# Order of weight sums, loads and block differences in the weight preparation of a hybrid decoder step

## The chip, the cores and the metric

The kernel runs on one core of one Trainium2 chip. The metric is the device time of one execution in microseconds (us). A core has a matrix engine (TensorE, PE), a vector engine (VectorE, DVE), a scalar engine (ScalarE, ACT), a general engine (GpSimd, POOL) and a sync engine (SyncE, SP), which here issues most transfers. Each engine executes its own instructions in order; between engines, semaphores order the work.

## The reference

One inference step of a one-layer decoder trunk, for a prompt group (512 tokens) and a sample group (8 x 8 tokens), 576 columns in all. D_MODEL is 1024, a branch is 512 wide, the MLP 4096.

```
h = _rmsnorm(x, g_mix_pre)
rq, rk, rv, rg, aq, ak, av, cb, cc, ch, gates = _split_in(h @ w_in)
o_ret, ret_new = _retention_branch(rq, rk, rv, rg, ret_s0)
if win_k is None:
    o_att, wk_new, wv_new = _attn_prompt(aq, ak, av, sinks)
else:
    o_att, wk_new, wv_new = _attn_sample(aq, ak, av, win_k, win_v, sinks)
o_conv, conv_new = _short_conv_branch(cb, cc, ch, conv_buf, conv_w)
branches = jnp.stack([o_ret, o_att, o_conv], axis=2)
proj = jnp.einsum('btnw,nwd->btnd', branches, w_branch)
gate = jax.nn.sigmoid(gates.reshape(b, t, N_BRANCH, d))
mixed = jnp.sum(gate * proj, axis=2) @ w_out
x = x + _rmsnorm(mixed, g_mix_post)
f = jnp.square(jax.nn.relu(_rmsnorm(x, g_ffn_pre) @ w_ff1)) @ w_ff2
x = x + _rmsnorm(f, g_ffn_post)
x = x + jax.nn.sigmoid(_rmsnorm(x, g_ple) @ w_ple_gate) * (p_l @ w_ple_proj)
```

## The kernel before

All activations are kept transposed, 576 columns in two halves of H = 288. Weights come as tiles W[j] of 128 x 1024 (eight 128 x 128 blocks, 512 KB). Each float32 operand is split into a rounded high part and the remainder, its low part: ACT casts the high part (`whi`, line 256), DVE subtracts it from the raw tile for the low part (`wlo`, line 257). A product is then three matmuls: high x high, high x low, low x high (`product`, line 329).

Most weights are used in pairs of tiles by Strassen's scheme with seven products instead of eight. A pair has four blocks of 128 x 512, b11, b12, b21, b22, and four sums of them:

```
t3 = b12 + b22      t2 = b11 + t3      t1 = b12 + b11      t4 = t2 + b21
```

For some pairs ("ready") the sums lie in DRAM already, summed there by accumulating transfers that POOL issues a few at a time after each `tick` (line 262 ff.); for the other pairs, here called plain, DVE adds them on the chip (line 227, 128 x 512, 90 instructions). `Pair.prep` is a generator with four pieces: b11 and t3; t2 and b21; t1 and b22; t4. Each piece loads, adds, casts, subtracts, and yields. For a plain pair the raw tile c holds W[j] = b12, b22 (512 KB), r holds b11, t3 and s holds t2, b21; t1 is written over b12 in c, t4 over t2 in s. The raw tiles rotate through four buffers (two pools of two).

The stream of products (`pair`, `pairs`) calls `step()` at fixed places, and each call advances the preparation of a coming tile by one piece. `pump()` does the same for the background work of the branches (retention, attention; lines 686 to 1040). A pair's products fill three PSUM banks: pa, pbb and pe. `value` (lines 418 to 427) reads two of the four results as differences: c21 = pe - hlf (line 424), c22 = hlf - pbb (line 426). The last product of a pair (b22) accumulates into pbb, so PE can begin it only after line 426 has read that bank. The order on each engine follows from the order of the program and the framework's scheduler, which honours priorities; the loads are issued by SP in its order, and each waits until its raw buffer is released.

Lines that the argument names: 390, 396, 400 copies of a pair on ACT; 424, 426 differences on DVE; 562, 690, 691 end of the retention's normalization on DVE, before which a power is taken on POOL (555) and read by 556; 721 a matmul that needs 690; 844 short convolution; 892 to 902 softmax of the sample attention, 1017 the transposes that need its result; 974 and 964 the same for the prompt.

Of the kernel before, what the change touches and what calls it, by code (L numbers as in the profile page):

```python
# [7 lines left out]
F32 = mybir.dt.float32  # L8
F32R = mybir.dt.float32r
AF = mybir.ActivationFunctionType  # L10
ALU = mybir.AluOpType
# [6 lines left out]
H = 288  # L18
# [66 lines left out]
def decoder_step(ctx: ExitStack, tc: tile.TileContext, xT, pT, W, consts, smalls, s0q, s0t, ckT, cv,  # L85
                 yT, o_rp, o_rs, o_akT, o_avT, o_ck, o_cv, o_conv):
    nc = tc.nc
    V, A, G, PE = nc.vector, nc.scalar, nc.gpsimd, nc.tensor
# [81 lines left out]
    def wtile(n):  # L170
        ph, pl = whi, wlo
        if n < 8:
            ph = pl = wparts[npart[0] % len(wparts)]
            npart[0] += 1
        return (ph.tile([P, n, P], F32R, tag="whi", name=nm("whi")), pl.tile([P, n, P], F32R, tag="wlo", name=nm("wlo")))
# [4 lines left out]
    def rawtile():  # L180
        pool = rawpools[nraw[0] % len(rawpools)]
        nraw[0] += 1
        return pool.tile([P, 8, P], F32, tag="wst", name=nm("wst"))
# [25 lines left out]
    def load(dst, src):  # L209
        nc.sync.dma_start(out=dst.rearrange("p k m -> p (k m)"), in_=src)  # L210

    class Pair:
# [7 lines left out]
        def prep(self, j):  # L220

            ready = j in sums
            t3, t2, t1, t4 = sums.get(j, [None] * 4)
            b12, b22, b11, b21 = [W[j + q // 2][:, Q * (q % 2):Q * (q % 2) + Q] for q in range(4)]

            def add(out, a, b):
                V.tensor_tensor(out=out, in0=a, in1=b, op=ALU.add)  # L227

            raw = []
            for i, parts in enumerate(((("b11", b11), ("t3", t3)), (("t2", t2), ("b21", b21)),  # L230
                                       (("t1", t1), ("b22", b22)), (("t4", t4),))):
                n = 4 * len(parts)
                if ready or i < 2:
                    r = rawtile()
                    raw.append(r)
                if ready:
                    for k, (name, src) in enumerate(parts):
                        load(r[:, 4 * k:4 * k + 4, :], src)
                elif i == 0:
                    c = rawtile()  # L240
                    load(c, W[j])
                    load(r[:, :4, :], b11)
                    add(r[:, 4:, :], c[:, :4, :], c[:, 4:, :])
                elif i == 1:
                    load(r[:, 4:, :], b21)
                    add(r[:, :4, :], raw[0][:, :4, :], raw[0][:, 4:, :])
                elif i == 2:
                    r = c
                    add(r[:, :4, :], r[:, :4, :], raw[0][:, :4, :])
                else:  # L250
                    r = raw[1]
                    add(r[:, :4, :], r[:, :4, :], r[:, 4:, :])
                hi, lo = wtile(n)
                for k, (name, _) in enumerate(parts):
                    self.w[name] = (hi, lo), 4 * k
                A.copy(out=hi, in_=r[:, :n, :])  # L256
                V.tensor_tensor(out=lo, in0=r[:, :n, :], in1=hi.bitcast(F32), op=ALU.subtract)  # L257
                if i % 2 == 0:
                    tick(hi)
                yield  # L260

    wsums = [weight_sums()]
    pace = cpool.tile([P, 1], F32, name="pace")
# [153 lines left out]
    def value(q, which, out):  # L417

        if which == "c11":
            return q.a[:, :H]  # L420
        if which == "c12":
            return q.b[:, :H]
        if which == "c21":
            V.tensor_tensor(out=out, in0=q.e[:, :H], in1=q.es, op=ALU.subtract)
        else:
            V.tensor_tensor(out=out, in0=q.es, in1=q.b[:, :H], op=ALU.subtract)  # L426
        return out

    def where(which):
# [186 lines left out]
    raw = []  # L616
# [728 lines left out]
    for c in range(1, 4):  # L1345
# [3 lines left out]
        n = 4 if c < 3 else 2  # L1349
# [140 lines left out]
```

## Time and profile before

| | before |
|---|---|
| three runs, median | 987.39 us (986.63 to 988.03) |
| the profiled execution | 987.22 us, span 985.4 us |
| PE busy | 957.6 us, 97% of the span, 7081 matmuls |
| DVE busy | 712.6 us, 72%, 1308 instructions |
| ACT busy | 531.5 us, 54% |
| POOL busy | 187.1 us |
| chain that ended last | PE 77%, DVE 13%, DMA 4%, ACT 2%, issue 2% |

The chain is followed back from the last instruction, at each step to what released it. PE's 77% of it is the part in which PE waited for nothing; the rest are places where the chain runs through other engines. A line in the profile is a line of the kernel; line 227 is the weight sum, 256 the cast, 257 the subtraction.

### The profile page before, as it was taken

How to read it: one execution, taken by the hardware profiler on the slowest of the kernel's cores; microseconds unless marked ns; L12 is line 12 of the kernel's file. 1: busy time of each engine (PE TensorE's matmuls, PEld its weight loads, DVE VectorE, ACT ScalarE, POOL GpSimd, SP SyncE). 2: the span in 40 equal slices, each digit the busy share in tenths (PEclk: the TensorE clock that was granted, in tenths of full speed). 3: DMA queues.
4: the chain of work that ended last, by engine and by line, in shares of the span. 5: the costliest groups of instructions: out<-in, count | busy, mean ns of one | idle time of the engine just before them, and what ended most of it. 6: DMA issues, size and time to landing. Idle time of an engine off the chain costs nothing.

```text
span 985.4 us, 18290 instructions
## 1 busy us (share of the span) xinstructions
PE 957.6 (97%) x7081; PEld 925.0 (94%) x7081; DVE 712.6 (72%) x1308; ACT 531.5 (54%) x1051; POOL 187.1 (19%) x257
## 2 busy tenths in 40 slices
PE   9999999989989999999999999999999999999998
PEld 9999898989979888799999999999999999999897
DVE  7898789765576776577427878558847965785986
ACT  7345444433345564545436455468558845885642
POOL 0414443433324222332001100000010011000010
PEclk9999999999999999999999999999999999999999
DMA  8637565658779665688522532444486368593112
GB/s 301 168 86 199 165 138 146 163 164 220 194 218 248 143 153 153 143 226 252 187 66 71 223 108 100 155 148 145 120 199 192 110 153 222 164 356 109 65 62 79
DMA packets 65576, 160.45 MB, mean 163 GB/s; under 512 B 8089, under 2 KB 11193, under 8 KB 64241
## 3 DMA queue, kind: packets, MB, share of 16 engines
q1 hardware_dynamic: 48672, 114.75, 34.9%
q0 software_dynamic: 16672, 44.48, 21.8%
q8 instruction: 55, 0.90, 0.4%
q14 instruction: 33, 0.26, 0.1%
q10 hardware_dynamic: 144, 0.06, 0.0%
HBM read 139.17 MB, written 51.55 MB: 194 GB/s over the span
## 4 chain that ended last, share of the span: by engine, by line
PE 77%; DVE 13%; DMA 4%; ACT 2%; issue 2%; POOL 1%; SPq 0%; ACTq 0%; DVEq 0%; POOLq 0%
PE pm L501 31%; PE pbb L329 18%; PE pa L329 12%; PE pe L329 12%; DMA wst<-in_W 3%; DVE wlo L257 3%; POOL rs_b L555 1%; DVE hlf L1149 1%; DVE xl L579 1%; DVE x L1150 1%; DVE wst L227 1%; DVE s L952 1%; PE pb L964 1%; ACT whi L256 1%; DVE wlo L164 1%
## 5 line engine op out<-in xcount | busy, mean ns | idle before, releaser
L257 DVE TENSOR_TENSOR wlo<-wst,whi 128x1024 fp32r<-128x1024 f32 (+1 forms) x180 | 195.4, 1087 | 95.9 <-ACT whi L256 95.1
L256 ACT CAST whi<-wst 128x1024 fp32r<-128x1024 f32 (+1 forms) x180 | 168.3, 940 | 129.9 <-PE pe L329 29.9
L329 PE MATMUL pbb<-xs,whi 128*128 128x288 f32 x1080 | 227.1, 302 | 10.0 <-DVE akv L426 4.1
L329 PEld LDWEIGHTS pbb<-xs,whi 128*128 128x128 f32 x1080 | 174.9, 190 | 19.0 <-DVE akv L426 4.9
L329 PE MATMUL pbb<-xs,wlo 128*128 128x288 f32 x540 | 160.6, 297 | 0.0
L329 PE MATMUL pa<-fq,whi 128*128 128x288 f32 x720 | 147.7, 297 | 0.6 <-DVE fq L583 0.5
L329 PEld LDWEIGHTS pa<-fq,whi 128*128 128x128 f32 x720 | 116.0, 189 | 2.3 <-DVE fq L583 0.7
L329 PE MATMUL pa<-fq,wlo 128*128 128x288 f32 x360 | 106.8, 297 | 0.4 <-DVE wlo L257 0.4
L329 PEld LDWEIGHTS pbb<-xs,wlo 128*128 128x128 f32 x540 | 102.7, 190 | 0.0
L163 ACT CAST whi<-wst 128x1024 fp32r<-128x1024 f32 (+1 forms) x64 | 61.5, 965 | 70.9 <-PE pm L501 48.8
L501 PE MATMUL pm<-xl,whi 128*128 128x288 f32 x384 | 95.0, 299 | 1.5 <-DVE xl L579 1.4
L501 PE MATMUL pm<-xh,whi 128*128 128x288 f32 x384 | 94.9, 300 | 1.5 <-ACT xh L578 1.4
L501 PE MATMUL pm<-xh,wlo 128*128 128x288 f32 x384 | 93.5, 296 | 0.3 <-DVE wlo L164 0.3
L164 DVE TENSOR_TENSOR wlo<-wst,whi 128x1024 fp32r<-128x1024 f32 (+1 forms) x64 | 71.2, 1118 | 23.7 <-ACT whi L163 21.3
L268 POOL COPY pace<-whi 128x1 f32<-128x1 f32 x61 | 36.6, 600 | 240.8 <-ACT whi L256 190.3
L227 DVE TENSOR_TENSOR wst<-wst 128x512 f32<-128x512 f32 x90 | 61.1, 686 | 28.7 <-DMA wst<-in_W 28.0
L555 POOL TENSOR_TENSOR rs_b<-rs_a,mhalf 128x9 f32<-128x9 f32 (+2 forms) x15 | 34.8, 2322 | 222.7 <-DVE rs_a L554 222.7
L329 PE MATMUL pe<-xs,whi 128*128 128x288 f32 x360 | 73.5, 294 | 0.1
L329 PE MATMUL pe<-fq,whi 128*128 128x288 f32 x360 | 73.3, 296 | 0.0
L501 PE MATMUL pm<-fq,whi 128*128 128x288 f32 x384 | 70.4, 296 | 0.0
L329 PEld LDWEIGHTS pa<-fq,wlo 128*128 128x128 f32 x360 | 67.9, 189 | 1.9 <-DVE wlo L257 1.1
L501 PEld LDWEIGHTS pm<-xh,whi 128*128 128x128 f32 x384 | 65.7, 188 | 3.9 <-ACT xh L578 2.4
(280 smaller groups left out, 2025.6 us busy)
## 6 DMA issues: line engine op xcount, KB each, us to landing
wst<-in_W SPq DMA_DIRECT2D x86, 512.0 KB, 4.5
wst<-in_W SPq DMA_DIRECT2D x105, 256.0 KB, 3.3
ts<-in_W POOLq DMA_DIRECT2D x90, 256.0 KB, 5.7
wst<-ts SPq DMA_DIRECT2D x60, 256.0 KB, 3.3
ts<-ts POOLq DMA_DIRECT2D x30, 256.0 KB, 3.5
df<-tmp POOLq DMA_DIRECT2D x16, 288.0 KB, 5.1
x<-in_xT SPq DMA_DIRECT2D x10, 288.0 KB, 4.2
dacc<-tmp SPq DMA_DIRECT2D x8, 288.0 KB, 4.3
```

The costliest lines, as they stand in the source:

```text
L163: A.copy(out=hi[:, c, :], in_=st[:, c, :])
L164: V.tensor_tensor(out=lo[:, c, :], in0=st[:, c, :], in1=hi[:, c, :].bitcast(F32), op=ALU.subtract)
L227: V.tensor_tensor(out=out, in0=a, in1=b, op=ALU.add)
L256: A.copy(out=hi, in_=r[:, :n, :])
L257: V.tensor_tensor(out=lo, in0=r[:, :n, :], in1=hi.bitcast(F32), op=ALU.subtract)
L268: t = G.tensor_copy(out=pace, in_=hi[:, 0, :1].bitcast(F32))
L329: PE.matmul(bank[:, :H], lhsT=lhs[:, s + j, :], rhs=rhs, start=start and j == 0 and i == 0, stop=j == 3 and i == 2, skip_group_check=True)
L501: PE.matmul(p[:, :H], lhsT=lhs[:, kw, :], rhs=r, start=s, stop=e)
L555: G.tensor_tensor(out=b, in0=a, in1=mhalf[:, :nb], op=ALU.pow)
L579: V.scalar_tensor_tensor(lo, src, gain(gi, k), hi.bitcast(F32), op0=ALU.mult, op1=ALU.subtract)
L952: V.scalar_tensor_tensor(s[:, h, :], dist, -SLOPES[h], p[g][:, i * w:i * w + w], op0=ALU.mult, op1=ALU.add)
L964: PE.matmul(po[grow(g), :], lhsT=avt[:, 128 * chunk + 64 * g:128 * chunk + 64 * g + 64], rhs=sb[g], start=kh == 0, stop=kh == nk - 1)
```

## The change

For the plain pairs the four pieces of `prep` are written out in another order; for the ready pairs nothing changes. All three raw buffers are taken at the start, in the order c, r, s, and all three loads are written there, W[j] first, then b11, b21. t2 and t1 are added before the subtraction of piece one, t4 before the subtraction of piece two; t4 is written over b11 in r instead of over t2 in s. The cast of t4 is written before the subtraction of piece three. In `value` both differences are issued with high priority.

```diff
--- before.py
+++ after.py
@@ -226,38 +226,49 @@
             def add(out, a, b):
                 V.tensor_tensor(out=out, in0=a, in1=b, op=ALU.add)
 
-            raw = []
-            for i, parts in enumerate(((("b11", b11), ("t3", t3)), (("t2", t2), ("b21", b21)),
-                                       (("t1", t1), ("b22", b22)), (("t4", t4),))):
-                n = 4 * len(parts)
-                if ready or i < 2:
+            def halves_of(r, *names):
+                n = 4 * len(names)
+                hi, lo = wtile(n)
+                for k, name in enumerate(names):
+                    self.w[name] = (hi, lo), 4 * k
+                A.copy(out=hi, in_=r[:, :n, :])
+                return lambda: V.tensor_tensor(out=lo, in0=r[:, :n, :], in1=hi.bitcast(F32), op=ALU.subtract), hi
+
+            if ready:
+                for i, parts in enumerate(((("b11", b11), ("t3", t3)), (("t2", t2), ("b21", b21)),
+                                           (("t1", t1), ("b22", b22)), (("t4", t4),))):
                     r = rawtile()
-                    raw.append(r)
-                if ready:
                     for k, (name, src) in enumerate(parts):
                         load(r[:, 4 * k:4 * k + 4, :], src)
-                elif i == 0:
-                    c = rawtile()
-                    load(c, W[j])
-                    load(r[:, :4, :], b11)
-                    add(r[:, 4:, :], c[:, :4, :], c[:, 4:, :])
-                elif i == 1:
-                    load(r[:, 4:, :], b21)
-                    add(r[:, :4, :], raw[0][:, :4, :], raw[0][:, 4:, :])
-                elif i == 2:
-                    r = c
-                    add(r[:, :4, :], r[:, :4, :], raw[0][:, :4, :])
-                else:
-                    r = raw[1]
-                    add(r[:, :4, :], r[:, :4, :], r[:, 4:, :])
-                hi, lo = wtile(n)
-                for k, (name, _) in enumerate(parts):
-                    self.w[name] = (hi, lo), 4 * k
-                A.copy(out=hi, in_=r[:, :n, :])
-                V.tensor_tensor(out=lo, in0=r[:, :n, :], in1=hi.bitcast(F32), op=ALU.subtract)
-                if i % 2 == 0:
-                    tick(hi)
-                yield
+                    low, hi = halves_of(r, *[name for name, _ in parts])
+                    low()
+                    if i % 2 == 0:
+                        tick(hi)
+                    yield
+                return
+
+            c, r, s = rawtile(), rawtile(), rawtile()
+            load(c, W[j])
+            load(r[:, :4, :], b11)
+            load(s[:, 4:, :], b21)
+            add(r[:, 4:, :], c[:, :4, :], c[:, 4:, :])
+            low, hi = halves_of(r, "b11", "t3")
+            add(s[:, :4, :], r[:, :4, :], r[:, 4:, :])
+            add(c[:, :4, :], c[:, :4, :], r[:, :4, :])
+            low()
+            tick(hi)
+            yield
+            low, _ = halves_of(s, "t2", "b21")
+            add(r[:, :4, :], s[:, :4, :], s[:, 4:, :])
+            low()
+            yield
+            low, hi = halves_of(c, "t1", "b22")
+            low4, _ = halves_of(r, "t4")
+            low()
+            tick(hi)
+            yield
+            low4()
+            yield
 
     wsums = [weight_sums()]
     pace = cpool.tile([P, 1], F32, name="pace")
@@ -420,10 +431,11 @@
             return q.a[:, :H]
         if which == "c12":
             return q.b[:, :H]
-        if which == "c21":
-            V.tensor_tensor(out=out, in0=q.e[:, :H], in1=q.es, op=ALU.subtract)
-        else:
-            V.tensor_tensor(out=out, in0=q.es, in1=q.b[:, :H], op=ALU.subtract)
+        with tc.high_priority():
+            if which == "c21":
+                V.tensor_tensor(out=out, in0=q.e[:, :H], in1=q.es, op=ALU.subtract)
+            else:
+                V.tensor_tensor(out=out, in0=q.es, in1=q.b[:, :H], op=ALU.subtract)
         return out
 
     def where(which):
```

Three places in DVE's order, as built. Line numbers of the changed kernel are higher: 235 is the subtraction (257 before), 438 and 436 are the differences (426 and 424), 574, 702, 703 are 562, 690, 691, and 904 to 914 are 892 to 902; 227 is the sum in both.

DVE, around 274 us. Before: wst515 holds the current pair's c; wst536 and wst535 are c and r of the next pair.

```order
L227 TENSOR_TENSOR wst535_3350<-wst536_3351 128x512
L227 TENSOR_TENSOR wst536_3351<-wst536_3351,wst535_3350 128x512
L257 TENSOR_TENSOR wlo529_3277<-wst515_3204,whi528_3276 128x1024
L426 TENSOR_TENSOR akv502_3102<-hlf507_3132,pbb505_3105 128x288
L227 TENSOR_TENSOR wst542_3383<-wst535_3350 128x512
L424 TENSOR_TENSOR akv502_3102<-pe506_3106,hlf507_3132 128x288
```

The same place after; wst514 is the current pair's c, and wst535, wst536, wst537 are c, r, s of the next.

```order
L227 TENSOR_TENSOR wst536_3351<-wst535_3350 128x512
L235 TENSOR_TENSOR wlo529_3278<-wst514_3203,whi528_3277 128x1024
L438 TENSOR_TENSOR akv502_3104<-hlf507_3134,pbb505_3107 128x288
L227 TENSOR_TENSOR wst535_3350<-wst535_3350,wst536_3351 128x512
L436 TENSOR_TENSOR akv502_3104<-pe506_3108,hlf507_3134 128x288
```

The second sum of the next pair (t1, in place in its c) stood ahead of the subtraction and the difference, and now stands behind both.

DVE, around 319 us, in the softmax of the sample attention. bgt577 and bgt578 are its two halves, mx, nmx, es, den their maxima, negated maxima, sink terms and sums. Before:

```order
L902 TENSOR_SCALAR bgt577_3618<-bgt577_3618,den582_3641 128x192 x2
L894 TENSOR_SCALAR nmx589_3711<-mx588_3710 128x2
L897 TENSOR_TENSOR es591_3713<-sm_118,nmx589_3711 128x2
L257 TENSOR_TENSOR wlo618_3896<-wst593_3739,whi617_3895 128x1024
L899 TENSOR_TENSOR den590_3712<-den590_3712,es591_3713 128x2
L900 RECIPROCAL den590_3712<-den590_3712 128x2
L902 TENSOR_SCALAR bgt578_3619<-bgt578_3619,den590_3712 128x192 x2
```

After, where wst635, wst636, wst637 are c, r, s of the next pair:

```order
L227 TENSOR_TENSOR wst636_4042<-wst635_4041 128x512
L914 TENSOR_SCALAR bgt577_3618<-bgt577_3618,den582_3641 128x192 x2
L904 TENSOR_REDUCE mx588_3710<-bgt578_3619 128x2
L235 TENSOR_TENSOR wlo618_3897<-wst592_3738,whi617_3896 128x1024
L905 TENSOR_TENSOR mx588_3710<-mx588_3710,sm_118 128x2
L227 TENSOR_TENSOR wst635_4041<-wst635_4041,wst636_4042 128x512
L906 TENSOR_SCALAR nmx589_3711<-mx588_3710 128x2
L227 TENSOR_TENSOR wst637_4043<-wst636_4042 128x512
L909 TENSOR_TENSOR es591_3713<-sm_118,nmx589_3711 128x2
```

Three sums of the next pair that stood behind the second line 902 now stand among the steps of the second half.

DVE, around 149 us, at the end of a normalization. Before:

```order
L560 SCALAR_TENSOR_TENSOR tmp298_1778<-rs_d301_1782,rs_b300_1781 128x512
L562 STREAM_TRANSPOSE bgt297_1777<-tmp298_1778 128x512
L690 TENSOR_TENSOR bgt302_1789<-pb273_1623,rg155_865 128x512
L717 TENSOR_TENSOR bgt315_1862<-pb313_1856,cst_122 128x2x128
L691 TENSOR_TENSOR ro194_1140<-bgt302_1789,bgt297_1777 128x4x128
```

After, with the t4 of a pair in wst322:

```order
L572 SCALAR_TENSOR_TENSOR tmp299_1782<-rs_d302_1786,rs_b301_1785 128x512
L227 TENSOR_TENSOR wst322_1932<-wst323_1933 128x512
L574 STREAM_TRANSPOSE bgt298_1781<-tmp299_1782 128x512
L702 TENSOR_TENSOR bgt303_1793<-pb274_1627,rg155_867 128x512
L729 TENSOR_TENSOR bgt317_1866<-pb315_1860,cst_122 128x2x128
```

The sum of t4 has moved up by nine rows and stands ahead of the transpose.

## Rows read from the trace of the kernel before

**Rows 1.** Windows: stretch, its length, busy us of each engine, PEclk, DMA share, GB/s.
```profile
200.00:300.00 100.00, 93.04 (x658) 88.60 (x657) 62.35 (x102) 38.41 (x66) 34.85 (x50) 0.97 0.74 203
500.00:985.00 485.00, 476.74 (x3534) 470.96 (x3532) 348.28 (x647) 290.15 (x585) 32.01 (x27) 1.00 0.47 143
```

**Rows 2.** PE's waits: waiter, line, releaser; us in total, times, longest us.
```profile
PE pb L721 <- DVE bgt L690: 5.3, 2, 2.9
PE pbb L329 <- DVE akv L426: 4.1, 1, 4.1
PE pbb L329 <- DVE tmp L426: 3.5, 2, 2.9
PE pbb L329 <- ACT pe L400: 2.4, 3, 1.5
...
PE pb L964 <- ACT bgt L974: 1.0, 2, 0.8
PE pb L1017 <- DVE bgt L902: 0.9, 1, 0.9
```

**Rows 3.** DVE's waits, the sums.
```profile
DVE wst L227 <- DMA wst<-in_W: 28.0, 14, 4.5
```

**Rows 4.** Windows behind three gaps of PE, at 209, 274 and 150 us.
```profile
209.96:213.37 3.41, 3.41 (x17) 3.41 (x16) 2.43 (x9) 2.47 (x5) 0.06 (x1) 0.50 0.01 4
274.80:278.21 3.41, 3.41 (x17) 3.41 (x16) 1.74 (x5) 1.17 (x2) 1.48 (x3) 0.50 0.83 273
150.20:153.60 3.40, 3.40 (x26) 3.40 (x27) 3.37 (x7) 0.44 (x2) 0.00 (x0) 1.00 0.38 130
```

**Rows 5.** DVE, timeline: start us, us, engine, line, operation, tiles [idle before <-releaser].
```profile
256.32 1.23 DVE L257 TENSOR_TENSOR wlo<-wst,whi 128x1024 fp32r<-128x1024 f32 x1 [0.25 <-ACT whi L256]
...
271.36 0.69 DVE L227 TENSOR_TENSOR wst<-wst 128x512 f32<-128x512 f32 x1 [3.15 <-DMA wst<-in_W]
272.09 0.69 DVE L227 TENSOR_TENSOR wst<-wst,wst 128x512 f32<-128x512 f32 x1
...
273.83 0.45 DVE L426 TENSOR_TENSOR akv<-hlf,pbb 128x288 f32<-128x288 f32 x1
```

**Rows 6.** PE, timeline at 274 us.
```profile
274.33 0.53 PE L329 MATMUL pbb<-xs,whi 128*128 128x288 f32 x2 [4.07 <-DVE akv L426]
```

**Rows 7.** SP's queue, the load of the sum at 271.36.
```profile
265.78 0.33 SPq L210 DMA_DIRECT2D wst<-in_W  x1
```

**Rows 8.** DVE, timeline at 207 us.
```profile
206.64 0.65 DVE L690 TENSOR_TENSOR bgt<-pb,rg 128x512 f32<-128x512 f32 x1
207.22 1.21 DVE L257 TENSOR_TENSOR wlo<-wst,whi 128x1024 fp32r<-128x1024 f32 x1
...
208.94 0.45 DVE L426 TENSOR_TENSOR tmp<-hlf,pbb 128x288 f32<-128x288 f32 x1
```

**Rows 9.** DVE, timeline at 380 us.
```profile
380.58 0.69 DVE L227 TENSOR_TENSOR wst<-wst 128x512 f32<-128x512 f32 x1 [2.83 <-DMA wst<-in_W]
```

**Rows 10.** DVE, timeline at 317 to 320 us.
```profile
317.03 0.69 DVE L257 TENSOR_TENSOR wlo<-wst,whi 128x512 fp32r<-128x512 f32 x1
...
319.54 0.16 DVE L894 TENSOR_SCALAR nmx<-mx 128x2 f32<-128x2 f32 x1
```

**Rows 11.** DMA issues: tiles, engine, count, KB each, median us to landing.
```profile
wst<-in_W SPq DMA_DIRECT2D x86, 512.0 KB, 4.5
wst<-in_W SPq DMA_DIRECT2D x105, 256.0 KB, 3.3
```

**Rows 12.** DVE, timeline at 118 and 146 us.
```profile
118.26 0.73 DVE L844 SCALAR_TENSOR_TENSOR tmp<-ubuf,sm,tmp 128x512 f32<-128x512 f32 x1
...
146.18 0.17 DVE L556 SCALAR_TENSOR_TENSOR rs_d<-rs_b 128x16 f32<-128x16 f32 x1 [2.83 <-POOL rs_b L555]
```

**Rows 13.** ACT, timeline at 92 us.
```profile
91.57 1.04 ACT L256 CAST whi<-wst 128x1024 fp32r<-128x1024 f32 x1 [2.90 <-DMA wst<-in_W]
```

**Rows 14.** SP's queue, the load that this cast waits for.
```profile
84.77 0.33 SPq L210 DMA_DIRECT2D wst<-in_W  x1
```

## The prediction

> **What bounds the kernel now.** I read the busy table first. Two stretches show where there is anything to win: from 500 us on TensorE (PE) is busy for 476.7 of 485 us at full clock, from 200 to 300 us for 93.0 of 100 at 0.97 [rows 1]. The table of PE's waits then gives the places. Six of its rows end on VectorE (DVE) or ScalarE (ACT) work that is itself queued among weight preparation: 5.3 us on L690 in two places (118 and 150 us), 4.1 us on L426 at 274 us, 3.5 us on L426 (2.9 of it at 209 us, 0.6 at 390 us), 2.4 us on L400 (1.5 of it at 93 us), 1.0 us on L974 and 0.9 us on L902 at 321 us [rows 2]. The third view, DVE's own waits, says why: it stands 28.0 us in 14 places on L227, a weight sum whose load has not landed [rows 3]. DVE executes in order, so whatever PE wants stands behind that sum.
>
> [...] At half speed 3.41 us do 1.7 us of work, so a drop costs 1.7 us.
>
> [...]
>
> **The change part by part.** The profiled execution took 987.22 us (span 985.4), 0.17 below the median of the runs; I sum against it and add the 0.17.
>
> *Same work.* A pair still has its four sums, its four casts and four subtractions, its three loads. Neither bytes nor sizes change, and PE's order stays but for some twenty small pieces. Past 500 us seven pairs are reordered too, but PE has next to no wait there; I count nothing, with the slack of those casts as cover.
>
> *All loads first; the sums ahead of the preceding subtraction.* A pair now takes its three buffers at once, and the buffer freed first goes to the 512 KB tile. So that load is issued earlier (8 us in the next item), while the 256 KB block b11 takes the buffer that is released last and is issued later. So the first sum waits less and the two sums that read b11 wait more.
>
> *274 us, the largest gain.* Before, the sum at 271.36 has waited 3.15 us for a load issued at 265.78; behind it come a second sum, one subtraction and L426 at 273.83, for which PE waits 4.07 us [rows 5 to 7]. In the new order the 512 KB load takes the buffer that the subtraction at 256.32 leaves at 257.6, so it has landed by then, and the second sum stands behind L426 (first listing in the section on the change). L426 moves by 3.15 plus one sum of 0.73 (start to start), or 3.9 us, to 269.95. Of the gap 0.2 is left and the drop after it goes: 3.9 + 1.7 = 5.6. Bounds: 3.2 (the sum moved, no clock returned, a part lost again) to 5.6.
>
> *209 us.* L690 at 206.64 is followed by a subtraction (207.22) and L691, and only then by L426 at 208.94 [rows 8]. With priority L426 follows L690 directly, so it starts at 207.22: 1.7 us, and with a gap of only 1.2 us left I take the clock back as well: 3.4. Bounds 1.7 to 3.4.
>
> *380 to 405 us.* A sum at 380.58 waits 2.83 us for its load [rows 9]. That load, too, is issued earlier now. Behind it lie a wait of 0.6 and two of together 1.0 on PE [rows 2]. I take 1.0 of these 1.6; bounds 0 to 1.6. Gains together: 5.6 + 3.4 + 1.0 = **10.0**.
>
> *321 us, the largest loss.* Here three sums of the next pair now stand ahead of the second softmax half (second listing): one before L892, one before L894 at 319.54, one before L897. The second reads b11, whose buffer is free only when the subtraction at 317.03 is done; the load is issued about 317.75 [rows 10]. With the median of 3.3 us [rows 11] it lands at 321.05, the sum takes 0.6 and L894 starts at 321.65: 2.1 us late, and L902, for which PE already waits 0.9, with it. Bounds: 0.7 (load landed in two microseconds) to 5.6 (6.8 us, below) plus a clock drop of 1.7.
>
> *150 us.* The last sum of a pair (0.69) now stands directly ahead of L562 and L690 (third listing). In addition one subtraction of 1.22 moves from 122 us into the crowded stretch 130 to 142 us, and the next pair's b11 comes later, so the statistics that POOL answers at 146.18 [rows 12] start late, by half of the 1.22 as I estimate: 1.3 together. Bounds 0.7 to 6.5 (that load late, and a clock drop).
>
> *118 us.* L844 (0.73, at 118.26 [rows 12]) now precedes L562 and L690: 0.7.
>
> *93 us.* ACT waits 2.90 us for a load that was issued at 84.77 and landed at 91.57, 6.8 us later [rows 13, 14]; L400 stands behind that cast. The load now waits for a subtraction that ends about 1.3 us later, behind a 512 KB load on SP's queue. With the same flight it is 1.3 worse, with the median of 3.3 us the wait of 1.5 vanishes. I take +0.5.
>
> *Small pieces at 62, 126 and 300 us* (a sum of 0.68 before a step that PE waits for; L730 behind two short differences; a load behind three others on SP): 0.9 together, 0 to 2. Losses together: 2.1 + 1.3 + 0.7 + 0.5 + 0.9 = **5.5**.
>
> Sum: 987.22 - 10.0 + 5.5 = 982.7, and 982.9 on the scale of the median.
>
> **The rivals.**
>
> *Late b11, slower.* The mechanism is one: b11 is requested last, and two sums that wait for it hold DVE's queue, at 150 and at 321 us. With a flight of f instead of 3.3 us both places lose f - 3.3 more, and both gaps become long enough for a clock drop (3.4 together). At f = 5.0: 5.5 + 2 x 1.7 + 3.4 = 12.3 against 10.0, so 987.39 + 2.3 = 989.7; at f = 6.8 (seen once, [rows 13, 14]) it would be 15.9 against 10.0, or 993.3. It decides from f of about 4 with both drops, 5.5 with none. For it speaks that 512 KB take 4.5 us [rows 11] and now go ahead on the same queue; against it that 3.3 is the median over 105 such loads, taken while others were in flight.
>
> *The wait moves, no change.* The number of raw buffers stays at four and every load in the trace is issued as its buffer is released. What L426 gains at 209 and 274 us (5.6 without the clock) would be lost again where PE, now earlier, meets DVE; left are 3.4 of clock and 1.0, against 5.5: 987.39 + 1.1 = 988.5. [...] The 28.0 us in 14 places [rows 3] agree with it, but of those 14 only the one at 274 us reached PE with more than a microsecond, which speaks against.
>
> *Only the gains, faster still.* The earlier loads give DVE slack, b11 never holds it, and of the losses only two operations directly ahead of L690 stay (0.7 + 0.7): 987.39 - 10.0 + 1.4 = 978.8.
>
> *The change does little.* The listings show that the differences move by one to three rows only; where such a row was not the last thing awaited, nothing happens. That is contained in the second rival.
>
> **How the numbers follow.** Forecast 0.43, late b11 0.20, moved wait 0.17, only gains 0.20. A measurement of this kernel can tell about 0.2% from no change, here 2 us: same is 985.4 to 989.4. Faster: forecast and only gains, 0.63; same: the moved wait, 0.17; slower: late b11, 0.20. The range goes from 977.5, just beyond the rival of only gains, to 990.5, which takes in the milder half of late b11; about 0.1 is left out above and less below.
>
> **What would show it.** Right: no wait on L426 over 1.5 us among PE's waits, and full clock after both places; DVE's 28.0 us on L227 fall, and sums wait for a 256 KB load instead of the 512 KB one; the wait on L902 grows from 0.9 to about 3 us; the two waits on L690 grow by 0.7 and 1.3. Wrong: a wait on L690 or L902 of over 5 us with a clock of 0.50 behind it (late b11); L426 early, but new waits of the same sum behind it (moved wait); a wait on a subtraction after 680 us, where I counted nothing.

## The result and the profile after

The changed kernel takes 991.91 us, median of 22 executions (988.27 to 995.56), the kernel before 986.62 us (980.99 to 992.0) beside it. The ratio is 1.0054, with an interval of 1.0041 to 1.0067: slower by 0.5%. The prediction was 982.9 us, faster. Single executions of either kernel differ by 4 us and more up and down, so I read two profiled executions of the kernel after: the first took 989.67 us (span 987.8), the second, `after_again`, 994.93 (span 993.0); before it was 987.22 (span 985.4). The median lies between the two.

**Stretches.** The windows of [rows 1] in the first profile after (columns as there):

```profile
200.00:300.00 100.00, 94.73 (x675) 89.15 (x674) 63.78 (x104) 39.89 (x68) 40.50 (x54) 0.99 0.77 214
500.00:985.00 485.00, 477.98 (x3545) 472.36 (x3544) 349.88 (x647) 291.19 (x587) 32.00 (x27) 1.00 0.47 143
```

From 200 to 300 us PE is busier by 1.7 us than in [rows 1] and its clock rose from 0.97 to 0.99. From 300 to 350 us it fell to 0.96. Past 500 us PE is busier by 1.2 us in 485, close to the nothing that was predicted.

**Waits.** PE's waits in the first profile after (as in [rows 2]); L340 is the product, L438 and L411 are lines 426 and 400 of before, L702, L722, L733, L914, L1029 are 690, 710, 721, 902, 1017:

```profile
PE pbb L340 <- ACT pe L411: 4.1, 4, 2.2
PE pb L733 <- ACT vt L722: 3.1, 1, 3.1
PE pb L733 <- DVE bgt L702: 2.9, 1, 2.9
PE pb L1029 <- DVE bgt L914: 2.1, 1, 2.1
PE pbb L340 <- DVE tmp L438: 1.8, 3, 1.1
```

The 4.07 us on `akv` are gone and the 2.9 on `tmp` have become 1.1. Two rows on ACT have grown: L411, which as L400 had 2.4 us, and L722, which takes the place of the 2.92 us on L690 at 150 us. What DVE and ACT themselves wait for:

```profile
DVE wst L227 <- DMA wst<-in_W: 38.0, 26, 3.8
...
ACT whi L234 <- DMA wst<-in_W: 27.8, 11, 4.8
```

Before, the row of the same casts and loads, L256 there, was:

```profile
ACT whi L256 <- DMA wst<-in_W: 7.9, 5, 2.9
```

DVE's waits on L227 were to fall from the 28.0 us of [rows 3]; they rose to 38.0. And the casts on ACT, of which the prediction looked at one, wait 27.8 us instead of 7.9. The chain that ended last fits that (shares of the span; before: PE 77%, DVE 13%, DMA 4%, ACT 2%):

```profile
PE 64%; DVE 15%; DMA 9%; ACT 6%; issue 3%; POOL 2%; SPq 0%; DVEq 0%; ACTq 0%; POOLq 0%
```

**Where the time went.** For each product I took its start after less its start before. This lag is level over long stretches; the difference of two levels is what the place between them gave or cost. Each profiled execution after against the one before, in us, a gain negative (rounded, so that a column may miss its sum by 0.1); places by the time before:

| place | predicted | first | second |
|---|---|---|---|
| 274 us | -5.6 | -5.6 | -5.6 |
| 209 us | -3.4 | -3.3 | -3.3 |
| 380 to 405 us | -1.0 | -1.7 | -1.7 |
| 321 us | +2.1 | +2.6 | -1.0 |
| 150 us | +1.3 | +0.1 | +3.2 |
| 118 us | +0.7 | +0.9 | +1.1 |
| 93 us | +0.5 | -0.8 | -0.8 |
| 83 us | none | +1.2 | +1.3 |
| 285 to 302 us | a part of 0.9 | +6.3 | +4.9 |
| 311 to 315 us | none | +0.2 | +5.9 |
| the rest, in pieces of under 1 us | 0 | +2.5 | +3.6 |
| whole execution | -4.5 | +2.3 | +7.6 |

The two large gains came in full, in both executions. They can be read off: L438 at 267.37 follows a subtraction at once, the second sum waits behind it, and PE runs through at full clock behind 274 and 209 us, where [rows 4] had 0.50 (DVE's timeline, then two windows):

```profile
266.22 1.23 DVE L235 TENSOR_TENSOR wlo<-wst,whi 128x1024 fp32r<-128x1024 f32 x1
267.37 0.45 DVE L438 TENSOR_TENSOR akv<-hlf,pbb 128x288 f32<-128x288 f32 x1
269.68 0.70 DVE L227 TENSOR_TENSOR wst<-wst,wst 128x512 f32<-128x512 f32 x1 [1.87 <-DMA wst<-in_W]
```

```profile
209.50:213.00 3.50, 3.06 (x23) 3.06 (x24) 3.45 (x10) 2.42 (x5) 0.00 (x0) 1.00 0.13 25
274.33:278.00 3.67, 3.67 (x22) 2.86 (x22) 0.00 (x0) 0.37 (x1) 0.40 (x1) 1.00 1.02 355
```

By 302 us the larger one was spent. PE stops at 285 and at 297 us, and the second time the clock falls to 0.59 for 3.39 us (PE's timeline, a window):

```profile
285.31 0.53 PE L340 MATMUL pbb<-xs,whi 128*128 128x288 f32 x2 [1.36 <-DVE aq L438]
...
297.01 0.54 PE L340 MATMUL pbb<-xs,whi 128*128 128x288 f32 x2 [2.25 <-ACT pe L411]
```

```profile
297.01:300.40 3.39, 3.39 (x16) 3.39 (x17) 2.63 (x3) 1.30 (x3) 3.03 (x5) 0.59 0.55 156
```

The first stop is not the late load. L438 stands behind a step of the retention, L821 (809 of before), which waited 4.58 us for an output transfer (DVE's timeline):

```profile
278.26 0.68 DVE L821 TENSOR_TENSOR bgt<-bgt,cst 64x512 f32<-64x512 f32 x1 [4.58 <-DMA out_o_rs<-bgt]
```

Before, its two steps together waited 1.6 us there; in e7 and e9 below, where t4 or the buffers lie otherwise, they waited 5.3 and 5.4 us, near the 5.7 of here, and PE stops there too, for 1.1 and 1.8 us. So it does not need the late load; that it comes of PE being earlier is argued. The second stop leads back to a load. On ACT the copy L411 stands behind a cast that waited 4.83 us (ACT's timeline):

```profile
295.61 1.04 ACT L234 CAST whi<-wst 128x1024 fp32r<-128x1024 f32 x1 [4.83 <-DMA wst<-in_W]
296.56 0.39 ACT L411 COPY pe<-pbb 128x288 f32<-128x288 f32 x1
```

That cast takes t2 and b21 of the coming pair (the pair of tile 42; L411 belongs to the pair of tile 40). Its b21 is the last row of SP's queue here, issued at 288.12:

```profile
284.92 0.33 SPq L162 DMA_DIRECT2D wst<-in_W  x1
285.30 0.43 SPq L997 DMA_DIRECT2D ckv<-in_ckT  x1
285.78 0.42 SPq L998 DMA_DIRECT2D ckv<-in_cv  x1
288.12 0.33 SPq L210 DMA_DIRECT2D wst<-in_W  x1
```

and DVE shows what it waited for, the subtraction of the earlier pair's t4, which ends at 288.09 (287.42 and 0.67):

```profile
287.42 0.67 DVE L235 TENSOR_TENSOR wlo<-wst,whi 128x512 fp32r<-128x512 f32 x1
```

This is the tile r: t4 is now written over b11, so r is released only when t4, the last piece of a pair, has been subtracted, and here the next pair's b21 takes that buffer. The framework hands out the four buffers by when they come free, so which load takes r differs along the kernel: as built, it is b21 where pairs follow each other (up to tile 24, tiles 38 to 42), and b11 where a single tile stands between two pairs (tiles 27 to 36 and 45 to 63). The cast began at 295.61, 7.5 us after the load was issued behind 1.5 MB that SP had issued in the 3.2 us before. While it was under way the core moved 343 GB/s, at a DMA share of 0.95:

```profile
288.10:295.60 7.50, 6.66 (x44) 5.51 (x42) 3.74 (x5) 1.31 (x4) 5.68 (x5) 1.00 0.95 343
```

In the kernel before, this b21 was issued at 288.38, no earlier, and the cast waited 1.75 us for it; but there PE came to the product it holds up 6.4 us later in the lag, so that wait cost nothing. The cover of the later load was PE's own delay at 274 us.

The second profile loses 4.9 us at this place, but mostly otherwise: L438 holds PE for 2.44 us behind the same step of the retention and the clock falls to 0.58 there, while the stop on L411 is 0.84 (PE's timeline):

```profile
289.54 0.85 PE L340 MATMUL pbb<-xs,whi 128*128 128x288 f32 x2 [2.44 <-DVE aq L438]
```

It has a larger loss behind it, at 311 to 315 us, which the first has not. A cast waits 6.52 us for the b11 of tile 45, issued at 305.87 as r of tile 42 came free; L411 stands behind the cast, PE stops for 3.19 us, and the clock falls to 0.50 (ACT's and PE's timelines, a window):

```profile
314.75 1.04 ACT L234 CAST whi<-wst 128x1024 fp32r<-128x1024 f32 x1 [6.52 <-DMA wst<-in_W]
```

```profile
317.07 0.85 PE L340 MATMUL pbb<-xs,whi 128*128 128x288 f32 x2 [3.19 <-ACT pe L411]
```

```profile
317.07:320.50 3.43, 3.43 (x14) 3.43 (x15) 2.70 (x6) 1.23 (x2) 1.00 (x2) 0.50 0.76 109
```

With PE so late, nothing was left to wait for at 321 us.

In the first profile the load of 288.12 (256 KB) took 7.5 us behind three of 512 KB, against a median of 3.3 [rows 11]. All four stood in SP's own queue.

### The profile page after: what moved, and what is told of

It is laid out like the page before. It is cut to its first block, busy times and chain, and to the rows that moved or that the text cites. A ratio compares the mean times of both kernels' runs of the same rounds, so it can differ in the third digit from the quotient of the medians.

```text
span 987.8 us, 18334 instructions
## 1 busy us (share of the span) xinstructions
PE 958.7 (97%) x7081; PEld 924.3 (94%) x7081; DVE 714.3 (72%) x1308; ACT 530.3 (54%) x1051; POOL 195.2 (20%) x257
## 4 chain that ended last, share of the span: by engine, by line
PE 64%; DVE 15%; DMA 9%; ACT 6%; issue 3%; POOL 2%; SPq 0%; DVEq 0%; ACTq 0%; POOLq 0%
PE pm L513 25%; PE pbb L340 15%; PE pe L340 10%; PE pa L340 10%; DMA wst<-in_W 7%; DVE wlo L235 3%; ACT whi L234 2%; DVE wlo L164 1%; DVE xl L591 1%; POOL rs_b L567 1%; DVE hlf L1161 1%; DVE x L1162 1%; DVE wst L227 1%; PE pb L976 1%; ACT s L908 1%
## 5 line engine op out<-in xcount | busy, mean ns | idle before, releaser
L340 PE MATMUL pbb<-xs,whi 128*128 128x288 f32 x1080 | 226.2, 302 | 9.2 <-ACT pe L411 4.1
L340 PEld LDWEIGHTS pbb<-xs,whi 128*128 128x128 f32 x1080 | 173.8, 189 | 19.7 <-ACT pe L411 6.1
L340 PE MATMUL pbb<-xs,wlo 128*128 128x288 f32 x540 | 160.3, 297 | 0.0
L340 PE MATMUL pa<-fq,whi 128*128 128x288 f32 x720 | 147.5, 296 | 1.2 <-ACT pbb L463 0.5
L340 PEld LDWEIGHTS pa<-fq,whi 128*128 128x128 f32 x720 | 115.6, 188 | 3.1 <-ACT pbb L463 1.3
L340 PE MATMUL pa<-fq,wlo 128*128 128x288 f32 x360 | 106.2, 295 | 0.0
L340 PEld LDWEIGHTS pbb<-xs,wlo 128*128 128x128 f32 x540 | 102.4, 190 | 0.0
L164 DVE TENSOR_TENSOR wlo<-wst,whi 128x1024 fp32r<-128x1024 f32 (+1 forms) x64 | 71.2, 1119 | 25.9 <-ACT whi L163 24.6
L279 POOL COPY pace<-whi 128x1 f32<-128x1 f32 x61 | 43.4, 712 | 234.7 <-ACT whi L234 182.2
L227 DVE TENSOR_TENSOR wst<-wst 128x512 f32<-128x512 f32 x90 | 61.8, 687 | 35.1 <-DMA wst<-in_W 34.0
L340 PE MATMUL pe<-fq,whi 128*128 128x288 f32 x360 | 73.8, 297 | 0.0
L340 PE MATMUL pe<-xs,whi 128*128 128x288 f32 x360 | 73.3, 294 | 0.1
L513 PEld LDWEIGHTS pm<-xl,whi 128*128 128x128 f32 x384 | 65.6, 188 | 4.1 <-DVE xl L591 3.8
```

What stands on the lines that cost most here:

```text
L164: V.tensor_tensor(out=lo[:, c, :], in0=st[:, c, :], in1=hi[:, c, :].bitcast(F32), op=ALU.subtract)
L279: t = G.tensor_copy(out=pace, in_=hi[:, 0, :1].bitcast(F32))
L340: PE.matmul(bank[:, :H], lhsT=lhs[:, s + j, :], rhs=rhs, start=start and j == 0 and i == 0, stop=j == 3 and i == 2, skip_group_check=True)
L513: PE.matmul(p[:, :H], lhsT=lhs[:, kw, :], rhs=r, start=s, stop=e)
```

## The experiments

All ratios are to the kernel before, run on the same chip. "r" and "s" are the raw tiles of b11 and of b21.

| run | what it is | ratio | interval |
|---|---|---|---|
| e1_prio | before, differences with priority | 0.9993 | 0.9977 to 1.0010 |
| e2_prep | after, without the priority | 1.0055 | 1.0035 to 1.0075 |
| e3_b11first | after, b11 loaded first | 1.0042 | 1.0027 to 1.0057 |
| e4_t4back | after, t4 in s and late, as before | 0.9965 | 0.9944 to 0.9985 |
| e4_again | the same once more | 1.0002 | 0.9977 to 1.0028 |
| e5_t4r_late | e4 with t4 in r | 1.0104 | 1.0062 to 1.0145 |
| e6_t4back_noprio | e4 without the priority | 0.9996 | 0.9976 to 1.0016 |
| e7_loadsfirst | e4 with t2 and t1 summed where before had them | 0.9975 | 0.9955 to 0.9995 |
| e7_again | the same once more | 0.9976 | 0.9955 to 0.9997 |
| e9_alloc | after, buffers taken in the order c, s, r | 1.0017 | 1.0000 to 1.0034 |
| e10_before_t4r | before with t4 in r | 1.0191 | 1.0157 to 1.0224 |

### The two halves of the change

**e1_prio**, the kernel before with

```diff
+        with tc.high_priority():
             if which == "c21":
```

> Only the priority of the two differences, everything else as before. Late small blocks (the losses of the change come from b11 and b21 being requested later): no loss arises, and at 209 us L426 follows L690 directly, wait 2.9 to 1.1 us and no clock drop, so about 3 us faster, 983.5 us, ratio 0.997; the 4 us at 274 us stay. Moved wait (what is won at one place is lost at the next): PE reaches 274 us 3 us earlier and waits 7 us there instead of 4, ratio 1.000.

It took 987.34 us against 987.72, so the 1.000 of the second reading (moved wait) and not the 0.997 of the first. In its profile the priority alone moves waits: against [rows 2], `akv` fell from 4.1 to 2.5, while `tmp` went from 3.5 in two places to 4.0 in three and the retention's end (L691 is 690 of before, L427 is 426) from 5.3 to 6.2.

**e2_prep**, the kernel after with those lines taken out again.

> Only the new preparation of pairs, differences without priority. Late small blocks: the gain at 274 us (wait 4 to 0) and all the losses stay, the gain at 209 us goes: about 3 us slower than the changed kernel, ratio 1.008 to before. Moved wait: PE comes later to 280 us and finds its data sooner, so no slower than the changed kernel, ratio 1.005.

993.0 us, the same as the kernel after. So the loss is in the preparation, and the priority is worth nothing that these runs can tell.

The moved wait expected 1.005 here, and it came, but not by the way that it named. At 209 us the first reading of both runs missed. The prediction put that gain down to the priority. But with the priority alone L427 still stands behind the subtraction, and PE waits 1.94 us; with the preparation alone L437 follows L701 (438 and 702 of after) directly, PE waits 1.08 as in the kernel after, and the 3.3 us of lag are gained (DVE's timelines, e1, then e2):

```profile
212.21 1.20 DVE L257 TENSOR_TENSOR wlo<-wst,whi 128x1024 fp32r<-128x1024 f32 x1
213.33 0.44 DVE L427 TENSOR_TENSOR tmp<-hlf,pbb 128x288 f32<-128x288 f32 x1
```

```profile
208.59 0.65 DVE L701 TENSOR_TENSOR bgt<-pb,rg 128x512 f32<-128x512 f32 x1
209.17 0.44 DVE L437 TENSOR_TENSOR tmp<-hlf,pbb 128x288 f32<-128x288 f32 x1
```

### Which load is late

**e3_b11first** takes buffers and issues loads in the order b11, W[j], b21:

```diff
-            c, r, s = rawtile(), rawtile(), rawtile()
-            load(c, W[j])
+            r, c, s = rawtile(), rawtile(), rawtile()
             load(r[:, :4, :], b11)
+            load(c, W[j])
```

> The changed kernel, but the buffers are taken and the loads written in the order b11, W[j], b21, as before. Late small blocks: b11 is no longer behind, the waits at 280 to 300 us shrink from 4.2 to about 1 us and the one on the softmax at 321 us from 2.1 to about 1, while W[j] is later again, so a part of the gain at 274 us goes (wait 2 us); ratio 0.998 to 1.000. Sums in the queue (the losses come from the sums standing ahead of other work, not from their loads): losses stay and the gain at 274 shrinks, ratio 1.006 to 1.008.

991.6 us: no gain, and DVE's waits on L227 grew to 49.7 us in 23 places. The order of the loads alone does not bring the time back. As built, the buffers go round otherwise here: where pairs follow each other, b11 takes the r of the pair before the last, so it is early, but W[j] takes the s of the pair just ahead, so it is late. The next runs bear on which buffer a load takes.

**e4_t4back** is the kernel after with t4 summed late and over t2 in s, as before:

```diff
-            add(r[:, :4, :], s[:, :4, :], s[:, 4:, :])
...
-            low4, _ = halves_of(r, "t4")
...
             yield
+            add(s[:, :4, :], s[:, :4, :], s[:, 4:, :])
+            low4, _ = halves_of(s, "t4")
             low4()
```

> The changed kernel, but t4 is written over t2 in s after the low part of t2, as before, so that r is released after the low part of b11 and t3. Late small blocks: the next pair's first loads find buffers earlier than in both kernels, the DMA waits of the sums fall below 28 us, ratio 0.996 to 0.998. Sums in the queue: only the 0.7 at 150 us and 0.6 at 62 us come back, ratio 1.003 to 1.004.

984.25 us in 5 executions, faster by the interval. It was repeated:

> The kernel with t4 back in s once more, on the chip of these runs, since it had 0.9965 from five runs only: 0.995 to 0.998 if that holds, and it stays the best of all; 0.999 to 1.001 if it was the chip.

985.42 us in 10 executions, 1.0002: no difference from before. The two intervals overlap. Between the two, e4's median rose by 1.2 us and that of the kernel before, on the two chips, fell by 2.1 (987.72, 985.6); whether e4 is a little faster than before stays open. What stands is that this one edit takes away the whole loss of 0.5%. It changes two things, where t4 lies and when it is summed.

**e5_t4r_late** takes these apart. It is e4 with t4 still late, but in r:

```diff
-            add(s[:, :4, :], s[:, :4, :], s[:, 4:, :])
-            low4, _ = halves_of(s, "t4")
+            add(r[:, :4, :], s[:, :4, :], s[:, 4:, :])
+            low4, _ = halves_of(r, "t4")
```

> The same order of work as the kernel with t4 back in s (ratio 0.9965), but t4 is written over b11 in r, as the change does; it is added after the low part of t2. Buffers (r is then the last of the three to be released, so the next pair's loads come late): most of the loss is back, ratio 1.002 to 1.005. Queue (what cost time was the sum of t4 standing ahead of the low part of t2): ratio 0.996 to 0.998.

997.63 us, 1.0104, by the medians slower than the kernel after (the intervals just meet). So the buffer makes the loss; the early sum of t4 rather helps once t4 lies in r, since the late one also reads, and holds, s. The b21 of tile 42, issued at 274.50 in e4's profile, is issued at 297.93 in that of e5. The edit also changes which buffers the next loads are given: where pairs follow each other, b11 mostly takes s of the pair ahead instead of its c. These two runs do not part that from the longer hold of r. PE's waits of e4, then of e5:

```profile
PE pbb L340 <- ACT pe L411: 6.0, 5, 2.5
...
PE pb L733 <- ACT vt L722: 1.4, 1, 1.4
```

```profile
PE pbb L340 <- ACT pe L411: 9.5, 6, 4.3
PE pb L733 <- ACT vt L722: 4.1, 1, 4.1
```

Both rows on ACT grow, and behind them are ACT's casts (e4, then e5):

```profile
ACT whi L234 <- DMA wst<-in_W: 20.3, 10, 4.6
```

```profile
ACT whi L234 <- DMA wst<-in_W: 30.8, 10, 5.9
```

**e9_alloc** keeps all sums where the change put them and takes the buffers in the order c, s, r. The loads keep their order, but each tile follows another one in its buffer.

```diff
-            c, r, s = rawtile(), rawtile(), rawtile()
+            c, s, r = rawtile(), rawtile(), rawtile()
```

> The changed kernel with the three buffers taken in the order c, s, r instead of c, r, s; nothing else, t4 stays in r and its sum ahead. By the addresses, where pairs follow each other (before 160 and 240 to 300 us) b21 then takes the buffer that c of the preceding pair left instead of that of its r, which is released last; where a single tile stands between pairs (160 to 240 and after 300 us) W[j] takes the buffer of r. Buffers: the waits on ACT's L411 at 280 to 300 us and on L722 at 150 us go, the softmax at 321 us stays or grows; ratio 0.998 to 1.002. Queue (the place of the sum of t4): 1.004 to 1.006 as the change.

987.2 us, 1.0017: two thirds of the loss are gone, without a single sum moved, and the wait on L722 is no longer among PE's waits of over 1.1 us. Now in a row of pairs b11 follows the earlier s and b21 the earlier c, which are released earlier than r. The b21 of tile 42 is issued at 282.79 instead of 288.12 (SP's queue), and the stop of PE on L411 between 280 and 300 us is gone:

```profile
282.79 0.33 SPq L210 DMA_DIRECT2D wst<-in_W  x1
```

The softmax at 321 us did not stay as expected, its wait is 0.7. In this profile PE is 5.2 us ahead of the kernel before at 440 us and loses that again behind it, 1.6 of it in a wait on L411 at 447 us; what is left of the loss is no longer the one at 297 us.

**e10_before_t4r** puts t4 into r in the kernel before:

```diff
-                    r = raw[1]
-                    add(r[:, :4, :], r[:, :4, :], r[:, 4:, :])
+                    r = raw[0]
+                    add(r[:, :4, :], raw[1][:, :4, :], raw[1][:, 4:, :])
```

> The kernel before, only t4 written over b11 in r instead of over t2 in s. By the addresses no load then takes the buffer of r from the pair directly ahead where pairs follow each other; with a single tile between them b21 takes r's buffer, as it took s's before, both released at the same moment. Buffers: no change, ratio 0.999 to 1.001, though t4 is in r as in the kernel that measured 1.0104. Against it, if writing t4 to another tile costs by itself (its read of two tiles, a longer hold of r): 1.003 to 1.010.

1004.69 us, 1.0191, the slowest of all; I had expected no change. There the buffers are taken in another order, and W[j] of the next pair takes the earlier s. The sum of t4 still reads s, late, so the largest load is held. At 144.64 that sum begins; the load that takes its buffer is issued at 145.35, as the sum ends, and the sum that needs it starts at 152.79, 7.4 us later (DVE's timeline and its waits):

```profile
144.64 0.68 DVE L227 TENSOR_TENSOR wst<-wst 128x512 f32<-128x512 f32 x1
...
152.79 0.69 DVE L227 TENSOR_TENSOR wst<-wst 128x512 f32<-128x512 f32 x1 [6.08 <-DMA wst<-in_W]
```

```profile
DVE wst L227 <- DMA wst<-in_W: 56.6, 21, 7.3
```

The miss agrees with e5 and e9 in what counts: which tile a load follows in its buffer, and which instruction reads that tile last. Here that is the sum of t4 itself. In e3 the loads take the same buffers, but t4 is summed earlier, and the ratio is 1.0042. I had looked only at who takes r.

### What is left when t4 lies in s

**e6_t4back_noprio**, e4 without the priority:

> The kernel with t4 back in s, and the differences without priority. Priority alone gave 0.9993 and its removal from the change gave 1.0055 against 1.0054, so if it is worth nothing here too: 0.9965 again. If the earlier loads leave DVE the slack in which priority counts: 0.998 to 1.000.

985.59 us, 0.9996, not to be told from e4 or from before.

**e7_loadsfirst** is e4 with t2 and t1 summed where the kernel before had them. Of the change it keeps the three loads ahead of everything and the priority:

```diff
             low, hi = halves_of(r, "b11", "t3")
-            add(s[:, :4, :], r[:, :4, :], r[:, 4:, :])
-            add(c[:, :4, :], c[:, :4, :], r[:, :4, :])
             low()
             tick(hi)
             yield
+            add(s[:, :4, :], r[:, :4, :], r[:, 4:, :])
             low, _ = halves_of(s, "t2", "b21")
...
+            add(c[:, :4, :], c[:, :4, :], r[:, :4, :])
             low, hi = halves_of(c, "t1", "b22")
```

> The kernel with t4 back in s, and t2 and t1 also added at their old places; of the change only the three loads at the start, W[j] first, and the priority remain. Buffers (the early, undisturbed loads are what brings 0.35%): ratio 0.996 to 0.998. Sums ahead (their place ahead of the low part of b11 and t3 is what brings it): ratio 0.999 to 1.001.

> The kernel after with t4 back over t2 in the b21 buffer and with the sums t2 and t1 at their old places, repeated. What stays of the change is the order of the loads (all three of a pair ahead of the earlier group's low part) and the priority. Theory Buffers (the time follows the buffer that a load takes and when it is released; the place of the sums is nearly free): within 0.2% of the kernel before, ratio 0.997 to 1.001, since the first look at 0.9975 carried the drift that the repeat of the t4-back kernel also showed (0.9965, then 1.0002). Theory Sums (the sums at their old places keep the DVE and ACT queues free and the earlier loads are a true gain): 0.9975 again, interval wholly below 1.

983.66 us against 986.23, then 982.48 against 985.87: 0.9975 and 0.9976, twice an interval below 1. This version is faster than the kernel before by a quarter of a per cent, and than the kernel after by about 0.8% (0.9976 over 1.0054). In its second profile (span 980.5) b21 of tile 42 is issued at 272.60, 15.5 us earlier than after, and the two stops of PE between 280 and 300 us have shrunk (SP's queue, PE's timeline):

```profile
272.60 0.33 SPq L210 DMA_DIRECT2D wst<-in_W  x1
```

```profile
283.26 0.53 PE L340 MATMUL pbb<-xs,whi 128*128 128x288 f32 x2 [1.11 <-DVE aq L438]
...
289.94 0.54 PE L340 MATMUL pbb<-xs,whi 128*128 128x288 f32 x2 [0.58 <-ACT pbb L401]
```

The lag against before is -1.8 us ahead of 274 us, -7.4 behind it, -5.3 at 302 us and -4.9 at the end: of the 5.6 us gained here some 3 reach the end, of those of the kernel after none. Whether it needs the priority I did not run apart; e1 and e6 speak against it. Nor is it shown that the early sums cost e4 anything against it; the two differ by about 0.2%, and their intervals overlap.

From the issue of a load on SP to the first product that uses it on PE (for W[j] that of t3), medians over the first 20 of the plain pairs, tiles 8 to 54 (us, one profiled execution each; e4 and e7 the first):

| kernel | b11 | W[j] | b21 | ratio |
|---|---|---|---|---|
| before | 32.7 | 26.9 | 26.4 | 1 |
| after | 22.9 | 33.4 | 25.5 | 1.0054 |
| e5 | 23.7 | 33.4 | 25.9 | 1.0104 |
| e10 | 29.4 | 23.7 | 27.1 | 1.0191 |
| e9 | 22.8 | 30.2 | 27.0 | 1.0017 |
| e4 | 19.1 | 31.0 | 29.7 | 0.9965, 1.0002 |
| e7 | 20.4 | 30.4 | 30.4 | 0.9975, 0.9976 |

Against before, the change gave W[j] 6.5 us of lead, at the cost of 10 on b11 and 1 on b21. The lead of b11, of which the prediction was afraid, does not order the kernels: it is shortest in e4 and e7. These two have the longest lead on b21. There and in the kernel before, s, the tile released last, goes to the pair after next where pairs follow each other, in after and e5 r goes to the very next. It is no law: in e9 and e3 r goes to the pair after next too, and both are behind e4.

A fifth raw buffer, the direct test of whether four are too few, wasn't tried.

## Why the prediction was wrong

**The gains were right in size, one of them by luck.** 274, 209 and 380 us gave 10.6 us in the lag against 10.0, with the clock at 1.00 behind the gaps at 274 and 209 us. The 1.7 us for a drop of the clock that two of these terms contain are an estimate from [rows 4], half of 3.41 us at 0.50; no run shows such a term by itself, the runs show the lags of 5.6 and 3.3 us, wait and clock together. At 274 us the reading of DVE's order held. At 209 us the number was right and its reason wrong: the priority was to bring it, but it comes without the priority (e2) and not in full from the priority alone (e1).

**The step that failed is "small pieces", 0.9 us, of which 300 us was one.** "A load behind three others on SP" was named there and given a fraction of a microsecond. The place from 285 to 302 us cost 6.3 us in the first profile. Of that the load's own part is some 4: the stop of 2.25 shown above and a clock at 0.59 for 3.39 us, about 1.6 in the lag by my estimate from these two. The rest are the stop of 1.36 behind the retention and one of 0.58 on L411 at 279 us (time after). Less the whole 0.9, the place makes 5.4 of the 7.0 us between the forecast for the profiled execution (982.7) and its time (989.67). Another 2.5 lie in small pieces that no run explains. In the second profile such a load, the b11 of tile 45, cost 5.9 at 311 to 315 us. The error behind it has four parts.

*The tile.* "b11 takes the buffer that is released last" holds only where a single tile stands between two pairs. Where pairs follow each other b21 takes it, which the prediction did not price at all.

*The cover.* I priced later loads at the places where a wait was near, and forgot that PE would come 6 us earlier to everything behind 274 us. A slack of before has to be taken less the gain that stands ahead of it.

*The queue.* The prediction followed b11 on DVE alone. The late loads show on ACT, 27.8 us in eleven places against 7.9, since a cast of t2 and b21 stands in ACT's order ahead of L411, which PE needs. In the second profile after, it is the wait at 150 us, where the cast holds L722, and here the clock falls too (ACT's timeline, a window):

```profile
151.87 1.04 ACT L234 CAST whi<-wst 128x1024 fp32r<-128x1024 f32 x1 [4.66 <-DMA wst<-in_W]
...
153.11 0.59 ACT L722 COPY vt<-pb 128x512 f32<-128x512 f32 x1
```

```profile
153.75:157.20 3.45, 3.45 (x15) 3.45 (x16) 3.42 (x7) 0.38 (x1) 0.00 (x0) 0.50 0.00 0
```

So the 1.3 us of 150 us were +0.1 in the first profile and 3.2 in the second, 1.1 of wait and the rest behind it, at the clock of 0.50.

*The flight.* I took 3.3 us, the median of [rows 11], for a 256 KB load. The median after is 3.5, but the loads that matter took, from issue to cast, 7.5 (issued at 288.12) and 7.2 (issued at 143.55, cast at 150.71), in the second profile 8.9 (issued at 305.87), near the 6.8 of [rows 13, 14]. The first two were each issued behind other loads on SP.

**321 us was right in size, its reason half right.** The wait on L914, line 902 of before, grew from 0.9 to 2.06 us, less than the 3 forecast, and a clock of 0.55 followed that was only in the bounds; together 2.6 in the lag against 2.1. And the sum that waited was the first of the three, for W[j], issued at 313.59, not the second, for b11, issued at 316.50 (DVE's and PE's timelines, a window):

```profile
318.96 0.69 DVE L227 TENSOR_TENSOR wst<-wst 128x512 f32<-128x512 f32 x1 [1.81 <-DMA wst<-in_W]
```

```profile
324.57 0.33 PE L1029 MATMUL pb<-cst,bgt 128*128 128x128 f32 x1 [2.06 <-DVE bgt L914]
```

```profile
324.57:328.00 3.43, 3.43 (x16) 3.34 (x17) 0.17 (x1) 1.06 (x2) 0.63 (x1) 0.55 0.66 86
```

**93, 118 and 83 us.** 93 us gave 1.3 us more than forecast, 118 us cost 0.2 more, 83 us was not forecast at all and cost 1.2; together next to nothing in the first profile.

**The rivals.** "Late b11, slower" had the sign and, at f = 6.8 to 7.5, the flight. It had the place and the load only in part: not b11 on DVE at 150 and 321 us, but whichever load of the next pair takes r, b21 or b11, on ACT as well as on DVE, and most of all behind the gain at 274 us. "The wait moves" is what happened there: L438 early, PE stopped again by 297 us. It let the gains of clock stand; the clock fell again at 297 and 324 us (to 0.59 and 0.55). That rival also named the four raw buffers. The runs agree in that the release of raw buffers bears on the time, but with four in every kernel the ratio went from 0.9975 to 1.0191 by which tile follows which and when it is released; what a fifth would do no run here shows.

**What is shown and what is argued.** That the loss comes from where t4 lies is shown (e4 against e5, one edit, with e10 as a second case), and that the sequence of buffers matters without any sum moved (e9). That PE's stop at 297 us comes from the load of 288.12 is read from the trace after; it fits e7 and e9, where that load is earlier (272.60, 282.79) and the stop is small or gone, and e5, where it is at 297.93 and the lag there rises by 7.5 us. No run changed that load alone. That PE's earlier arrival took away the cover, for this load and for the step of the retention, is read from the traces and argued; no run tests it by itself. What the early sums of t2 and t1 do by themselves, and why e9 loses behind 440 us, stays open.

## What to carry to other kernels

Ask of every tile in a rotating pool who takes its buffer next and which instruction releases it last: writing a result over a tile that would have been free can hold the next load (here the b21 of tile 42, issued at 297.93 in e5 and at 274.50 in e4), at a cost that no instruction of the change shows (1.0104 in e5, 0.9965 and 1.0002 in e4). The flight of a load that will stand in a burst is to be taken from such loads (here 7.2 and 7.5 us), not from the median (3.3 before, 3.5 after), and a wait that it causes is to be followed on each engine that reads the tile. And where a change makes the bottleneck engine earlier by some microseconds, every slack behind that place that is measured against this engine shrinks by as much; here that is argued, for the 6.4 us at 297 us.

## What the hardware showed that was not expected

From issue to the cast that waited for it, a 256 KB load took 7.2 and 7.5 us in a burst, against a median flight of 3.3 to 3.5, and 8.9 in the second profile. During the one of 7.5 us the core moved 343 GB/s.

The clock fell after shorter gaps of PE than those of [rows 4], and not always after longer ones. Behind gaps of 2.25 and 2.06 us (297 and 324 us) it was 0.59 and 0.55 for 3.4 us; behind 3.06 us at 152.59 it stayed at 1.00 in the first profile after, and behind 3.60 us at the same place it was 0.50 in the second.

Single executions of one kernel spread over 11 us before and 7 us after. A ratio of 0.9965 from five executions was not repeated with ten; 0.9975 from ten was, with twelve.
